# The output product of a SwiGLU as a 2 by 2 block product with seven multiplications, its partial sums kept in PSUM

## The chip, the cores and the metric

The kernel runs on one core of one Trainium2 chip. The metric is device time in microseconds (us) for one execution; the median of three executions stands for a kernel. The profile is of one more execution, so it has a time of its own.

## The reference

One decoder layer on 512 tokens of width 1024, all in float32. What matters here is the second of its two SwiGLU half steps:

```
h = h + 0.5 * swiglu(rmsnorm(h, norm_ffn2), ffn2_w1, ffn2_w3, ffn2_w2)

def swiglu(x, w1, w3, w2):
    return (silu(x @ w1) * (x @ w3)) @ w2        # w1, w3: 1024 x 2816, w2: 2816 x 1024
```

Before it come a first SwiGLU, an attention (NSA) and a state space mixer (S5); after it a gated input embedding and a last norm.

## The kernel before

**Layout.** Everything is kept transposed: `h` is 8 row tiles of 128 features by 512 tokens. The 2816 hidden features are 22 tiles (`FT_N`). A weight reaches SBUF as a *unit* of 128 by 1024 float32 (`unit`, 512 KB), which `split` (L154) divides in a high and a low part: ScalarE casts (L159), VectorE subtracts (L160). Every product is then made of three float32r matmuls, high by high, high by low, low by high (`mm3`). One matmul is a weight load of 128 by 128 and a pass of the moving operand, 256 or 512 columns (tokens). All of them are issued in one line, L134.

**Up.** Tile 0 of the second SwiGLU is computed plainly. The 21 others go through `up_fast`: seven products of half size, each 12 matmuls of 256 columns, in place of eight, with sums carried on in PSUM from a copy (L400 copies a partial sum from a bank of tag A into one of tag B, on which the next matmuls accumulate). That is 84 matmuls of 256 columns for a tile. The hidden tile (128 x 512) is written by VectorE in two halves (L423, L427), multiplied by the silu (L433) and split by `hidden` (L353 on ScalarE, L354 on VectorE) into a tile of tag `hq`, of which there are seven.

**Down.** `down` takes a group of hidden tiles (`CHUNKS`: 6, 6, 5, 5). For each of the 8 output tiles m it runs three matmuls of 512 columns for every hidden tile of the group into a bank of tag C, and L487 adds half of the bank to `h[:, m]` on VectorE. A group's `down` comes after the first `up` of the next group.

**PSUM** has eight banks of 128 x 512 float32: two each of the tags A, B, C, D, used in turn.

**Order.** Each engine executes its instructions in an order written out by hand for the whole kernel (`ENGINE_ORDER`: steps between the numbers that the instructions have in the program; `TILE_ORDER`: some reuses of tiles). `impose` turns it into dependencies. Three matmuls of one product mostly stay together, and products of neighbouring steps are mixed.

**Weights ahead.** Eight units can be in SBUF during the second SwiGLU: four of the ring and four of `fp2` (`more[:] = fp2, 4`).

Of the kernel before, what the change touches and what calls it, by code (L numbers as in the profile page):

```python
# [24 lines left out]
CHUNKS = [range(0, 6), range(6, 12), range(12, 17), range(17, 22)]  # L25
UNIT = 1024
# [10 lines left out]
def _ffn_order():  # L37

    order = []
    for c, fl in enumerate(CHUNKS):  # L40
        order.append(("up", fl[0]))
        if c:
            order.append(("down", c - 1))
        order.extend(("up", f) for f in fl[1:])
    order.append(("down", len(CHUNKS) - 1))
    return order


FFN_ORDER = _ffn_order()


def _unit_widths():

    w = []

    def ffn():
        for kind, i in FFN_ORDER:
            w.extend([UNIT, UNIT] if kind == "up" else [UNIT] * len(CHUNKS[i]))

    ffn()  # L60
    w.extend([UNIT] * 12)
    w.extend([840, 840, 560])
    w.extend([UNIT] * 8)
    w.extend([UNIT] * 2)
    w.extend([UNIT] * 8)
    w.extend([UNIT] * 2)
    ffn()
    w.extend([UNIT] * 8)
    return w
# [7 lines left out]
def block_kernel(ctx: ExitStack, tc: tile.TileContext, a: dict, out: bass.AP):  # L77
# [267 lines left out]
    def ffn(nrm, done, plain, xp, hp, fp, bg=None, first=None, restate=None):  # L345
        fast = not bg
        if True:
            hid = {}

            def hidden(f, t3):  # L350
                hq = hp.tile([128, 2, SEQ], FR, tag="hq", name="hq")
                hh, hl = hq[:, 0], hq[:, 1]
                S.copy(hh, t3)  # L353
                V.tensor_tensor(hl, t3, hh.bitcast(F32), OP.subtract)  # L354
                hid[f] = (hh, hl)
# [52 lines left out]
            def up_fast(f, after):  # L408
# [13 lines left out]
                t3 = fp.tile([128, SEQ], F32, tag="t3", name="t3")  # L422
# [13 lines left out]
            def up(f):  # L436
                if f >= plain:
                    return up_fast(f, f + 1 < FT_N and f not in [c[0] for c in CHUNKS[1:]])
# [19 lines left out]
                t3 = fp.tile([128, SEQ], F32, tag="t3", name="t3")  # L458
# [36 lines left out]

            for kind, i in FFN_ORDER:
                if kind == "up":
                    up(i)
                    aside(SMALL.get(i, int(i > 7)))
                else:  # L500
                    down(CHUNKS[i], i == len(CHUNKS) - 1)
# [847 lines left out]
    hp2 = x2.enter_context(tc.tile_pool(name="hid2", bufs=7, reuse_waits="tile"))  # L1349
# [17 lines left out]

    pled = dram.tile([D_MODEL, SEQ], F32, tag="pled", name="pled")
    norm2 = rsqrt_steps([n2.acc], 4)
    for m in range(KT):  # L1370
# [3 lines left out]
        for k in range(2):  # L1374
# [6 lines left out]
            if (m, k) == NORM_AT[1]:  # L1381
                _, pb2 = next(norm2)
                n2.spread(lambda: hp2.tile([128, 2, SEQ], F32, tag="hq", name="xn"), xpool, x2pool, pb2)
        et = fp2.tile([128, SEQ], F32, tag=("t1", "t3")[m % 2], name="et")
        S.copy(et, o)
        nc.sync.dma_start(pled[128 * m:128 * m + 128], et)
    more[:] = fp2, 4
    ffn(n2, feed_next(3), N_PLAIN, x2pool, hp2, fp2)
# [5 lines left out]
    with tc.tile_pool(name="gate", bufs=2, reuse_waits="tile") as gp:  # L1394
# [62 lines left out]
N_PLAIN = 1  # L1457
NORM_AT = (2, 0), (4, 1)
# [366 lines left out]
```

## Time and profile before

| | |
|---|---|
| median of 3 executions | 1035.49 us (1035.15 to 1035.61) |
| profiled execution | 1035.68 us |
| its span, first to last instruction | 1033.8 us |
| TensorE busy | 1017.7 us, 98% of the span |
| VectorE busy | 808.9 us, 78% |
| ScalarE busy | 522.7 us, 51% |
| mean granted TensorE clock | 0.995 of full speed |

TensorE's busy time counts overlapping matmuls once, and a matmul's duration is longer than the distance from its start to the next one's. So the distance, and not the duration, says what a matmul costs in a full stream.

### The profile page before, as it was taken

The numbers are of one execution on the slowest core, as the hardware profiler recorded it, in microseconds if no ns is written. First come the engines' busy times: TensorE is split into PE (matmuls) and PEld (weight loads), VectorE is DVE, ScalarE is ACT, GpSimd is POOL, SyncE is SP. The second block draws the span as 40 slices with busy tenths as digits, with TensorE's granted clock in tenths as the row PEclk, the third lists the DMA queues.
The fourth block names the chain that finished last, engine by engine and source line by source line (L and its number), as shares of the span: only waits on it lengthen the run. The fifth ranks groups of instructions, "written<-read, shape, count | busy, mean of one in ns | idle before, by whom it ended". The sixth has DMA issues, their size and how long they took to land.

```text
span 1033.8 us, 16693 instructions
## 1 busy us (share of the span) xinstructions
PE 1017.7 (98%) x6362; PEld 894.6 (87%) x6362; DVE 808.9 (78%) x1351; ACT 522.7 (51%) x915; POOL 82.2 (8%) x102
## 2 busy tenths in 40 slices
PE   9999999999999999999999999999999999999995
PEld 8788899889999878897687687998999899899885
DVE  7999997778897777899799979774576467476676
ACT  6364365346435521348779847552455255255452
POOL 1000111001011020000000000111011011110000
PEclk9999999999999999999999999999999999999998
DMA  8526366757755838986610174557265545544312
GB/s 312 135 73 177 78 185 164 224 125 157 212 145 123 285 101 214 279 241 143 224 41 1 25 222 120 133 149 198 62 153 155 131 116 144 149 107 119 102 62 82
DMA packets 76257, 151.66 MB, mean 147 GB/s; under 512 B 19473, under 2 KB 32913, under 8 KB 75921
## 3 DMA queue, kind: packets, MB, share of 16 engines
q1 hardware_dynamic: 63792, 130.26, 41.1%
q0 software_dynamic: 11520, 20.16, 12.1%
q8 instruction: 50, 0.82, 0.3%
q10 hardware_dynamic: 864, 0.17, 0.1%
q14 instruction: 31, 0.25, 0.1%
HBM read 123.53 MB, written 17.30 MB: 136 GB/s over the span
## 4 chain that ended last, share of the span: by engine, by line
PE 92%; DVE 4%; DMA 1%; issue 1%; ACT 0%; POOL 0%; DVEq 0%; SPq 0%; POOLq 0%
PE ps_C L134 28%; PE ps_B L134 25%; PE ps_A L134 24%; PE ps_D L134 15%; DVE lo L160 1%; DMA raw<-in_wpack 1%; DVE acc L192 1%; DVE xn L283 1%; DVE xn L298 0%; DVE xl L290 0%; DMA h<-in_xT 0%; PE ps_C L685 0%; ACT hi L159 0%; POOL ri L325 0%; PE ps_D L938 0%
## 5 line engine op out<-in xcount | busy, mean ns | idle before, releaser
L159 ACT CAST hi<-raw 128x1024 fp32r<-128x1024 f32 (+2 forms) x206 | 213.5, 1043 | 251.2 <-PE ps_C L134 95.5
L160 DVE TENSOR_TENSOR lo<-raw,hi 128x1024 fp32r<-128x1024 f32 (+2 forms) x206 | 247.2, 1211 | 57.8 <-ACT hi L159 56.1
L134 PE MATMUL ps_C<-hq,hi 128*128 128x512 f32 x704 | 218.2, 391 | 0.0
L134 PEld LDWEIGHTS ps_C<-hq,hi 128*128 128x128 f32 x704 | 127.2, 188 | 22.7 <-issue 0.2
L134 PE MATMUL ps_C<-hq,lo 128*128 128x512 f32 x352 | 137.1, 389 | 0.0
L134 PE MATMUL ps_A<-xh,lo 128*128 128x256 f32 (+1 forms) x432 | 134.1, 310 | 0.9 <-DVE lo L160 0.9
L134 PE MATMUL ps_A<-xh,hi 128*128 128x256 f32 (+1 forms) x432 | 134.6, 311 | 0.0
L134 PE MATMUL ps_A<-xl,hi 128*128 128x256 f32 (+1 forms) x432 | 134.3, 311 | 0.1
L134 PEld LDWEIGHTS ps_A<-xl,hi 128*128 128x128 f32 x432 | 81.6, 189 | 6.0 <-DVE xl L290 0.5
L134 PEld LDWEIGHTS ps_A<-xh,lo 128*128 128x128 f32 x432 | 81.7, 189 | 5.6 <-DVE lo L160 1.4
L134 PEld LDWEIGHTS ps_A<-xh,hi 128*128 128x128 f32 x432 | 81.5, 189 | 5.7 <-issue 0.5
L134 PE MATMUL ps_B<-sh,hi 128*128 128x256 f32 x304 | 85.9, 283 | 0.0
L134 PE MATMUL ps_B<-sh,lo 128*128 128x256 f32 x304 | 85.3, 281 | 0.5 <-DVE lo L160 0.5
L134 PE MATMUL ps_B<-sl,hi 128*128 128x256 f32 x304 | 85.5, 281 | 0.0
L487 DVE SCALAR_TENSOR_TENSOR h<-ps_C,h 128x512 f32<-128x512 f32 x64 | 44.1, 689 | 47.6 <-PE ps_C L134 46.9
L134 PEld LDWEIGHTS ps_C<-hq,lo 128*128 128x128 f32 x352 | 66.1, 188 | 14.2
L134 PE MATMUL ps_D<-sl,hi 128*128 128x256 f32 x236 | 66.5, 282 | 0.5 <-DVE sl L302 0.5
L134 PE MATMUL ps_D<-sh,hi 128*128 128x256 f32 x236 | 66.4, 281 | 0.0
L134 PE MATMUL ps_D<-sh,lo 128*128 128x256 f32 x236 | 66.2, 280 | 0.0
L369 POOL DMA_DIRECT2D raw<-raw x38 | 32.8, 862 | 397.0 <-DVE lo L160 364.7
L363 POOL DMA_DIRECT2D raw<-in_wpack x38 | 35.8, 942 | 300.9 <-DVE h L1122 131.1
L134 PEld LDWEIGHTS ps_B<-sh,hi 128*128 128x128 f32 x304 | 57.3, 188 | 0.9 <-ACT pu L384 0.2
(401 smaller groups left out, 2313.5 us busy)
## 6 DMA issues: line engine op xcount, KB each, us to landing
raw<-in_wpack SPq DMA_DIRECT2D x171, 512.0 KB, 4.0
raw<-in_wpack POOLq DMA_DIRECT2D x38, 256.0 KB, 5.0
raw<-raw POOLq DMA_DIRECT2D x38, 256.0 KB, 3.3
so<-s5o SPq DMA_DIRECT2D x8, 512.0 KB, 6.6
h<-in_xT SPq DMA_DIRECT2D x8, 256.0 KB, 4.9
s5f<-fs SPq DMA_DIRECT2D x4, 512.0 KB, 4.2
s5o<-gt SPq DMA_DIRECT2D x4, 512.0 KB, 3.7
s5t<-tcs SPq DMA_DIRECT2D x2, 1024.0 KB, 5.2
```

The lines of the kernel that those rows point to most:

```text
L134: return PE.matmul(o, lhsT, rhs, start=start, stop=stop, **kw)
L159: S.copy(hi[:, c], raw[:, c])
L160: V.tensor_tensor(lo[:, c], raw[:, c], hi[:, c].bitcast(F32), OP.subtract)
L192: adder.tensor_tensor(self.acc, self.acc, sq, OP.add)
L283: V.scalar_tensor_tensor(row(k), h[:, k, :], gains[:, self.gi, k:k + 1], pb, OP.mult, OP.mult)
L363: nc.gpsimd.dma_start(a0[:, 1], src[:, 0:512], accum_op=OP.add)
L369: nc.gpsimd.dma_start(a1[:, 1], a0[:, 1], accum_op=OP.add)
L487: V.scalar_tensor_tensor(h[:, m, :], o, 0.5, h[:, m, :], OP.mult, OP.add)
```

## The change

The 16 first hidden tiles of the second SwiGLU are put in four groups of four, the last six are a group as before (`CHUNKS2`).

For a group of four, `down_block` computes output tiles m and m + 4 together, as a 2 by 2 block product: rows (m, m + 4), columns of w2's input (even hidden tiles, odd ones), tokens (0 to 255, 256 to 511). It needs seven products instead of eight, each of 2 hidden tiles x 3 = 6 matmuls of 256 columns. VectorE forms three sums of weight blocks (`sw`), which are split like the weights (`v`), and one block is overwritten in place.

The hidden tiles come in pairs: `target` puts the two halves of two tiles in one tile `st`, `pair` adds four sums of them on VectorE, and the seven blocks are split together (1792 columns, one cast on ScalarE, one subtraction on VectorE) into a tile `hs` of tag `hq`. That tag has two tiles of 3584 columns in place of seven of 1024.

In PSUM a row tile uses a half bank X of tag A, a half bank W of tag D, and two banks P and Q, which are both banks of tag C and stay the same for all 16 row tiles. X is copied three times by ScalarE while it grows: into P's first half, Q's first half, P's second half, and further products are accumulated on the copies. One matmul for P and one for Q stand ahead of the first row tile. Half of W, Q, X and P is then added to `h` by four instructions of VectorE instead of two.

`begin` of the next but one hidden tile comes ahead of the group's last row tile. Weights are kept six units ahead instead of eight (`more[:] = fp2, 2`), and the temporaries of the norm before it lie in the new tiles (`spare`). `ENGINE_ORDER` and `TILE_ORDER` are new for the whole kernel.

```diff
+CHUNKS2 = [range(0, 4), range(4, 8), range(8, 12), range(12, 16), range(16, 22)]
...
+            def target(f):
+                if not nblock:
+                    return fp.tile([128, SEQ], F32, tag="t3", name="t3")
+                if f >= blocked or f % 2 == 0:
+                    keep["st"] = fp.tile([128, 7, 256], F32, tag="st", name="st", bufs=1)
+                i = 0 if f >= blocked else 2 * (f % 2)
+                return keep["st"][:, i:i + 2].rearrange("p a b -> p (a b)")
+
+            def pair(f):
+                s = keep["st"]
+                V.tensor_tensor(s[:, 4], s[:, 1], s[:, 0], OP.subtract)
+                V.tensor_tensor(s[:, 1], s[:, 3], s[:, 1], OP.subtract)
+                V.tensor_tensor(s[:, 5], s[:, 4], s[:, 3], OP.subtract)
+                V.tensor_tensor(s[:, 6], s[:, 5], s[:, 2], OP.add)
+                hs = hp.tile([128, 2, 7, 256], FR, tag="hq", name="hs")
+                S.copy(hs[:, 0], s)
+                V.tensor_tensor(hs[:, 1], s, hs[:, 0].bitcast(F32), OP.subtract)
+                hid[f - 1] = hs
...
+            def down_block(fl):
+                hs = [hid[f] for f in fl[::2]]
...
+                for m in range(mh):
+                    raw = unit(True)
+                    a_ = raw.rearrange("p (q c) -> p q c", q=4)
+                    sw = fp.tile([128, 3, 256], F32, tag=("pp", "ph")[m % 2], name="sw", bufs=1)
+                    V.tensor_tensor(sw[:, 0], a_[:, 2], a_[:, 3], OP.add)
+                    V.tensor_tensor(sw[:, 1], a_[:, 0], sw[:, 0], OP.subtract)
+                    V.tensor_tensor(a_[:, 2], a_[:, 0], a_[:, 2], OP.subtract)
+                    V.tensor_tensor(sw[:, 2], a_[:, 1], sw[:, 1], OP.add)
+                    w = split(raw)
+                    v = [fp.tile([128, 768], FR, tag=n, name=n, bufs=2) for n in ("vh", "vl")]
+                    swf = sw.rearrange("p q c -> p (q c)")
+                    S.copy(v[0], swf)
+                    V.tensor_tensor(v[1], swf, v[0].bitcast(F32), OP.subtract)
...
+                    def prod(o, u, q, slot, begin, end):
+                        for j in range(2):
+                            c = slice(256 * q + 128 * j, 256 * q + 128 * j + 128)
+                            for i, (x_, y_) in enumerate(((0, 0), (0, 1), (1, 0))):
+                                mm(o, u[x_][:, c], hs[j][:, y_, slot], begin and j + i == 0,
+                                   end and j == 1 and i == 2, skip_group_check=True)
+
+                    if m == mh - 1:
+                        for _ in begin(fl[-1] + 2):
+                            pass
+                    X, W = bank("A")[:, lo], bank("D")[:, lo]
+                    prod(X, w, 0, 0, True, True)
+                    prod(W, w, 2, 1, True, True)
+                    S.copy(P[:, lo], X)
+                    prod(X, v, 1, 5, False, True)
+                    prod(P[:, lo], w, 1, 2, False, True)
+                    S.copy(Q[:, lo], X)
+                    prod(X, v, 0, 4, False, True)
+                    prod(Q[:, lo], w, 3, 6, False, True)
+                    S.copy(P[:, hi], X)
+                    prod(P[:, hi], v, 2, 3, False, True)
+                    g = h[:, m + mh].rearrange("p (a t) -> p a t", a=2)
+                    V.scalar_tensor_tensor(g, W[:, None, :].to_broadcast([128, 2, 256]), 0.5, g, OP.mult, OP.add)
+                    for t, o in ((lo, Q[:, lo]), (hi, X)):
+                        V.scalar_tensor_tensor(h[:, m + mh, t], o, 0.5, h[:, m + mh, t], OP.mult, OP.add)
+                    V.scalar_tensor_tensor(h[:, m], P, 0.5, h[:, m], OP.mult, OP.add)
...
-    hp2 = x2.enter_context(tc.tile_pool(name="hid2", bufs=7, reuse_waits="tile"))
+    hp2 = x2.enter_context(tc.tile_pool(name="hid2", bufs=2, reuse_waits="tile"))
...
-    more[:] = fp2, 4
-    ffn(n2, feed_next(3), N_PLAIN, x2pool, hp2, fp2)
+    more[:] = fp2, 2
+    ffn(n2, feed_next(3), N_PLAIN, x2pool, hp2, fp2, None, None, None, CHUNKS2, FFN_ORDER2, NBLOCK)
```

## Rows read from the trace of the kernel before

**Rows 1.** The page's part 1: the span, and for each engine the busy time, its share of the span and its instructions.

```profile
span 1033.8 us, 16693 instructions
PE 1017.7 (98%) x6362; PEld 894.6 (87%) x6362; DVE 808.9 (78%) x1351; ACT 522.7 (51%) x915; POOL 82.2 (8%) x102
```

**Rows 2.** The waits of TensorE in the whole run, longest first: who waited for whom, us in total, times, longest.

```profile
PE ps_D L134 <- DVE dg L331: 3.3, 2, 2.6
...
PE ps_D L134 <- DVE sl L302: 0.5, 1, 0.5
PE ps_B L134 <- DVE lo L160: 0.5, 1, 0.5
...
```

**Rows 3.** Busy time of each engine in stretches of 20 us of the second SwiGLU and in the last 33.8 us: PE, PEld (weight loads), DVE, ACT, POOL, each with its instructions (x), then the granted clock, the DMA share and GB/s.

```profile
660.00:680.00 20.00, 20.00 (x169) 19.88 (x168) 15.57 (x22) 11.82 (x20) 2.62 (x3) 1.00 0.64 152
740.00:760.00 20.00, 20.00 (x171) 19.98 (x170) 17.11 (x23) 12.32 (x21) 3.52 (x4) 1.00 0.57 145
880.00:900.00 20.00, 20.00 (x98) 16.85 (x97) 9.78 (x12) 4.45 (x5) 2.60 (x3) 1.00 0.63 176
1000.00:1033.80 33.80, 22.56 (x146) 20.00 (x144) 20.84 (x45) 10.96 (x22) 1.56 (x2) 0.85 0.19 63
```

**Rows 4.** The chain that ended last, pieces of it inside the second SwiGLU: start, length in us, what. ps_C is a run of matmuls of 512 columns (`down`), ps_B and ps_D runs of 256 columns (`up_fast`).

```profile
809.41 8.18 PE ps_C L134 x36
...
857.78 2.13 PE ps_D L134 x18
859.91 2.84 PE ps_B L134 x24
...
882.14 8.87 PE ps_C L134 x39
```

**Rows 5.** VectorE's groups from 640 to 965 us by shape: line, engine, operation, out<-in, count, then busy us, mean ns of one, and the idle time before them with its releasers.

```profile
L160 DVE TENSOR_TENSOR lo<-raw,hi 128x1024 fp32r<-128x1024 f32 x85 | 102.7, 1222 | 36.8 <-ACT hi L159 36.4
L487 DVE SCALAR_TENSOR_TENSOR h<-ps_C,h 128x512 f32<-128x512 f32 x28 | 19.3, 690 | 35.2 <-PE ps_C L134 35.2
L354 DVE TENSOR_TENSOR hq<-t,hq 128x512 fp32r<-128x512 f32 x22 | 15.2, 689 | 4.8 <-ACT hq L353 4.2
L366 DVE TENSOR_TENSOR raw<-raw 128x512 f32<-128x512 f32 x21 | 14.4, 688 | 0.4
L372 DVE TENSOR_TENSOR al<-raw,ah 128x512 fp32r<-128x512 f32 x21 | 14.4, 687 | 8.6 <-ACT ah L371 8.3
L433 DVE TENSOR_TENSOR t<-t,t 128x512 f32<-128x512 f32 x21 | 14.4, 687 | 2.9 <-ACT t L432 2.8
L365 DVE TENSOR_TENSOR raw<-raw 128x512 f32<-128x512 f32 x20 | 13.8, 689 | 0.4
L423 DVE TENSOR_TENSOR t<-ps_D,pu 128x256 f32<-128x256 f32 x21 | 8.8, 421 | 10.8 <-PE ps_D L134 9.0 <-ACT pu L384 1.8
L427 DVE TENSOR_TENSOR t<-p,ps_B 128x256 f32<-128x256 f32 x21 | 8.8, 419 | 10.0 <-PE ps_B L134 9.8
```

**Rows 6.** VectorE's instructions in order of time where they follow each other without a gap (start, us, line, operation, out<-in, count of a merged run).

```profile
638.88 2.48 DVE L298 TENSOR_TENSOR xn<-xn 128x512 f32<-128x512 f32 x4
...
644.16 3.48 DVE L160 TENSOR_TENSOR lo<-raw,hi 128x1024 fp32r<-128x1024 f32 x3
...
664.59 0.42 DVE L423 TENSOR_TENSOR t<-ps_D,pu 128x256 f32<-128x256 f32 x1
664.92 2.35 DVE L160 TENSOR_TENSOR lo<-raw,hi 128x1024 fp32r<-128x1024 f32 x2
```

**Rows 7.** ScalarE's groups from 640 to 965 us, columns as in rows 5.

```profile
L159 ACT CAST hi<-raw 128x1024 fp32r<-128x1024 f32 x85 | 88.5, 1050 | 100.0 <-PE ps_C L134 56.9 <-PE ps_B L134 17.3 <-issue 16.8
L353 ACT CAST hq<-t 128x512 fp32r<-128x512 f32 x22 | 13.7, 621 | 14.0 <-DVE t L433 12.8 <-DVE t L461 1.2
...
L400 ACT COPY ps_B<-ps_A 128x256 f32<-128x256 f32 x21 | 7.6, 364 | 9.1 <-PE ps_A L134 8.9
```

**Rows 8.** Instructions in order of time around a wait of TensorE for VectorE, start and us; in brackets the idle time before and its releaser.

```profile
641.89 2.35 DVE L302 TENSOR_TENSOR sl<-xn,sh 128x1024 fp32r<-128x1024 f32 x2
...
642.38 0.28 PE L134 MATMUL ps_D<-sh,hi 128*128 128x256 f32 x1
643.16 0.19 PEld L134 LDWEIGHTS ps_D<-sl,hi 128*128 128x128 f32 x1 [0.81 <-DVE sl L302]
643.16 0.38 PE L134 MATMUL ps_D<-sl,hi 128*128 128x256 f32 x1 [0.50 <-DVE sl L302]
...
643.38 0.28 PE L134 MATMUL ps_D<-sh,lo 128*128 128x256 f32 x1
```

**Rows 9.** The last matmul of a product and the copy of its result by ScalarE, which was waiting for it.

```profile
666.76 0.28 PE L134 MATMUL ps_B<-sh,lo 128*128 128x256 f32 x1
...
667.12 0.37 ACT L384 COPY pu<-ps_B 128x256 f32<-128x256 f32 x1 [0.37 <-PE ps_B L134]
```

More of the change, by code (lines that the diff above doesn't have):

```diff
@@ L32, with _ffn_order @@
 NCH = NG // GC
-def _ffn_order():
+def _ffn_order(chunks):
     order = []
-    for c, fl in enumerate(CHUNKS):
+    for c, fl in enumerate(chunks):
         order.append(("up", fl[0]))
@@ L44, in _ffn_order, with ffn @@
         order.extend(("up", f) for f in fl[1:])
-    order.append(("down", len(CHUNKS) - 1))
+    order.append(("down", len(chunks) - 1))
     return order
-FFN_ORDER = _ffn_order()
+FFN_ORDER = _ffn_order(CHUNKS)
+FFN_ORDER2 = _ffn_order(CHUNKS2)
 def _unit_widths():
     w = []
[L56 to L60, printed above, removed]
+    def ffn(order, chunks):
+        for kind, i in order:
+            w.extend([UNIT, UNIT] if kind == "up" else [UNIT] * len(chunks[i]))
+    ffn(FFN_ORDER, CHUNKS)
     w.extend([UNIT] * 12)
@@ L66, in _unit_widths @@
     w.extend([UNIT] * 2)
-    ffn()
+    ffn(FFN_ORDER2, CHUNKS2)
     w.extend([UNIT] * 8)
@@ L342, in block_kernel, with ffn @@
     G.memset(negh, -0.5)
-    def ffn(nrm, done, plain, xp, hp, fp, bg=None, first=None, restate=None):
+    def ffn(nrm, done, plain, xp, hp, fp, bg=None, first=None, restate=None, chunks=CHUNKS, order=FFN_ORDER, nblock=0):
         fast = not bg
@@ L348, in ffn @@
             hid = {}
-            def hidden(f, t3):
-                hq = hp.tile([128, 2, SEQ], FR, tag="hq", name="hq")
+            keep = {}
+            blocked = chunks[nblock][0] if nblock else 0
+            def target(f):
[15 more added lines that the diff above has]
+                hid[f - 1] = hs
+            def hidden(f, t3):
+                if f < blocked:
+                    if f % 2:
+                        pair(f)
+                    return
+                if nblock:
+                    r = (f - blocked) % 3
+                    if r == 0:
+                        keep["hs"] = hp.tile([128, 3584], FR, tag="hq", name="hq")
+                    hq = keep["hs"][:, 1024 * r:1024 * r + 1024].rearrange("p (a t) -> p a t", a=2)
+                else:
+                    hq = hp.tile([128, 2, SEQ], FR, tag="hq", name="hq")
                 hh, hl = hq[:, 0], hq[:, 1]
@@ L421, in up_fast @@
                 t1 = fp.tile([128, SEQ], F32, tag="t1", name="t1", bufs=2 if fast else 1)
-                t3 = fp.tile([128, SEQ], F32, tag="t3", name="t3")
+                t3 = target(f)
                 V.tensor_tensor(t3[:, lo], zw, pu, OP.subtract)
@@ L437, in up @@
                 if f >= plain:
-                    return up_fast(f, f + 1 < FT_N and f not in [c[0] for c in CHUNKS[1:]])
+                    return up_fast(f, f + 1 < FT_N and f not in [c[0] for c in chunks[1:]])
                 wu = [first if f == 0 and first else unit(), unit()]
@@ L457, in up @@
                 t1 = fp.tile([128, SEQ], F32, tag="t1", name="t1", bufs=2 if fast else 1)
-                t3 = fp.tile([128, SEQ], F32, tag="t3", name="t3")
+                t3 = target(f)
                 if fast:
@@ L494, in down @@
                         aside((2 - m % 2) * (m > 4 or fl[0] > 0))
-            for kind, i in FFN_ORDER:
-                if kind == "up":
+            def down_block(fl):
+                hs = [hid[f] for f in fl[::2]]
+                if "P" not in keep:
+                    for n in "PQ":
+                        keep[n] = bank("C")
+                P, Q = keep["P"], keep["Q"]
+                mh = KT // 2
+                for m in range(mh):
[11 more added lines that the diff above has]
+                    V.tensor_tensor(v[1], swf, v[0].bitcast(F32), OP.subtract)
+                    if "C" not in keep:
+                        keep["C"] = True
+                        for o in (P, Q):
+                            mm(o, w[0][:, :128], nrm.xh[:, 0], True, True, skip_group_check=True)
+                    def prod(o, u, q, slot, begin, end):
[23 more added lines that the diff above has]
+                    V.scalar_tensor_tensor(h[:, m], P, 0.5, h[:, m], OP.mult, OP.add)
@@ L498, in ffn @@
+            for kind, i in order:
+                if kind == "down" and i < nblock:
+                    down_block(chunks[i])
+                elif kind == "up":
                     up(i)
@@ L500, in ffn @@
                 else:
-                    down(CHUNKS[i], i == len(CHUNKS) - 1)
+                    down(chunks[i], i == len(chunks) - 1)
     fd = dram.tile([128, NG, 128], F32, tag="s5f", name="s5f")
@@ L1366, in block_kernel, with spare @@
     n2 = state["n"]
+    def spare():
+        ts = [hp2.tile([128, 3584], F32, tag="hq", name="xn") for _ in range(2)]
+        ts.append(fp2.tile([128, 1792], F32, tag="st", name="xn", bufs=1))
+        views = [t[:, 1024 * r:1024 * r + 1024].rearrange("p (a t) -> p a t", a=2)
+                 for t, n in zip(ts, (3, 3, 1)) for r in range(n)]
+        views.append(views[4])
+        return lambda: views.pop(0)
     pled = dram.tile([D_MODEL, SEQ], F32, tag="pled", name="pled")
@@ L1382, in block_kernel @@
                 _, pb2 = next(norm2)
-                n2.spread(lambda: hp2.tile([128, 2, SEQ], F32, tag="hq", name="xn"), xpool, x2pool, pb2)
-        et = fp2.tile([128, SEQ], F32, tag=("t1", "t3")[m % 2], name="et")
+                n2.spread(spare(), xpool, x2pool, pb2)
+        et = fp2.tile([128, SEQ], F32, tag=("t1", "vh")[m % 2], name="et")
         S.copy(et, o)
         nc.sync.dma_start(pled[128 * m:128 * m + 128], et)
-    more[:] = fp2, 4
-    ffn(n2, feed_next(3), N_PLAIN, x2pool, hp2, fp2)
+    more[:] = fp2, 2
+    ffn(n2, feed_next(3), N_PLAIN, x2pool, hp2, fp2, None, None, None, CHUNKS2, FFN_ORDER2, NBLOCK)
     del more[:]
@@ L1457 @@
 N_PLAIN = 1
+NBLOCK = 4
 NORM_AT = (2, 0), (4, 1)
@@ L1695, in half_tiles, with quarters, ffn @@
                                 .transpose(1, 0, 2) for t, hf in zip(ws, hs)], axis=1))
-    def ffn(w1, w3, w2, plain=FT_N):
-        for kind, i in FFN_ORDER:
+    def quarters(w, fl):
+        for m in range(KT // 2):
+            add(np.concatenate([w[k * 128:(k + 1) * 128, o * 128:(o + 1) * 128]
+                                for o in (m, m + KT // 2) for ks in (fl[::2], fl[1::2]) for k in ks], axis=1))
+    def ffn(w1, w3, w2, plain, chunks, order, nblock=0):
+        for kind, i in order:
             if kind == "up" and i >= plain:
@@ L1703, in ffn @@
                 up_tile(w3, i)
-            else:
-                m_major(w2, range(KT), CHUNKS[i])
-    ffn(x["ffn1_w1"][0], x["ffn1_w3"][0], x["ffn1_w2"][0], PLAIN1)
+            elif i < nblock:
+                quarters(w2, chunks[i])
+            else:
+                m_major(w2, range(KT), chunks[i])
+    ffn(x["ffn1_w1"][0], x["ffn1_w3"][0], x["ffn1_w2"][0], PLAIN1, CHUNKS, FFN_ORDER)
     w_in = x["w_in"][0]
@@ L1735, in _pack_weights @@
     m_major(x["w_ple"][0], range(8), range(2))
-    ffn(x["ffn2_w1"][0], x["ffn2_w3"][0], x["ffn2_w2"][0], N_PLAIN)
+    ffn(x["ffn2_w1"][0], x["ffn2_w3"][0], x["ffn2_w2"][0], N_PLAIN, CHUNKS2, FFN_ORDER2, NBLOCK)
     m_major(x["w_ple_gate"][0], range(8), range(8))
```

328 rows, old and new, of tables (ENGINE_ORDER, TILE_ORDER) are left out of this document.

## The prediction

> **What bounds the kernel now.** I read the page's busy times first, then the waits of TensorE, then the second SwiGLU in slices, then the spacing of its matmuls. TensorE is busy 1017.7 of 1033.8 us [rows 1], and its longest waits are a few us outside the two SwiGLUs; in the second one only two of 0.5 us are left, both at its very start [rows 2]. From there to the end of its work TensorE fills every slice, 20.00 of 20.00 us at full clock, in the stretches of `up` and in those of `down` alike [rows 3]. So time is gained there only by a shorter stream of matmuls, and any wait that the change puts into this stream is lost one for one. The last row of [rows 3] shows the tail, where TensorE works 22.56 of 33.80 us; the change doesn't shorten it.
>
> A matmul costs its distance to the next one, not its duration. The chain gives it as a run's length by its count [rows 4]: with 512 columns 8.18 / 36 = 0.2272 us and 8.87 / 39 = 0.2274; with 256 columns 2.13 / 18 = 0.1183 and 2.84 / 24 = 0.1183. Two halves cost 0.2366, so cutting a pass in two costs 4%.
>
> **The matmuls.** Removed: for 16 hidden tiles, 8 output tiles and 3 parts, 384 matmuls of 512 columns, 384 x 0.2273 = 87.3 us. Added: 16 row tiles x 7 products x 6 matmuls = 672 of 256 columns, 672 x 0.1183 = 79.5 us, and the two that stand ahead of P and Q, of 512 columns, 0.5 us. Balance: -7.3 us. The last six hidden tiles cost 144 matmuls of 512 columns either way, and the 21 tiles of `up_fast` the same 84 each. If the distances are off by 0.0005 us in the worst direction, the balance lies between -6.8 and -7.8.
>
> **The copies of X.** This is the wait that the change adds. X can grow only when ScalarE has read it. Between the last matmul of X and the next one into X (or into the half that was copied to) stand the six of another product, in places more: counted along TensorE's new list, 30 of the 48 copies have exactly six between, the 18 others nine or more. With six, the next one is due 7 x 0.1183 = 0.83 us after X's last matmul started. The row for such a step: ScalarE's copy starts 0.36 us after the last matmul's start (666.76 to 667.12) and takes 0.37 us [rows 9]; a copy from PSUM to PSUM takes 0.364 [rows 7]. Then TensorE. Its restart after a wait is in [rows 8]: the first of VectorE's two subtractions, 1.21 us each, ends at 643.10; weight load and matmul start together at 643.16, and the next matmul comes 0.22 us later instead of 0.118. So the dependent matmul counts as started 0.06 + 0.10 = 0.16 us after its releaser. Sum: 0.36 + 0.37 + 0.16 = 0.89 us against 0.83 due: 0.06 us lost at each of the 30, 1.8 us, if ScalarE stands idle when X is complete. The bounds: 0, if the restart costs nothing because the wait is over when the weight load is due; and a cast of 1.05 us [rows 7] that has just begun on ScalarE when X is complete, for which I give a price in the rivals. In the new list most casts stand behind a copy and not between two of a row tile, so I take 1.8.
>
> P's half is another such ring: the first copy of a row tile writes where VectorE has to have read the row tile before it. P's last matmul, 0.36 us, 0.60 us on VectorE, then 0.36 for the copy and 0.16: 1.5 us, against 13 x 0.118 = 1.54 due. No loss if VectorE takes P at once.
>
> **VectorE.** Its price in a full stream is again the distance. Four of 512 columns take 2.48 us and the last of them 0.69, so (2.48 - 0.69) / 3 = 0.60; three of 1024 take 3.48, so (3.48 - 1.22) / 2 = 1.13; one of 256 is 664.59 to 664.92, 0.33 [rows 6]. About 0.07 + 0.00104 per column; by that (an estimate) 768 columns cost 0.87 and 1792 cost 1.93. An `up` tile has three of 1024, five of 512 and two of 256 [rows 5]: 3.39 + 3.00 + 0.66 = 7.05 us, in 84 x 0.1183 = 9.94 us of TensorE. After the change L354 goes (-0.60), and each pair adds four of 256 and one of 1792, 3.25 us: 8.08 us a tile on average, 9.70 on an odd one. A row tile of `down_block`: four of 256 for the sums (1.32), 1.13 and 0.87 for the splits, two of 512 and two of 256 for `h` (1.86): 5.18 us, against 42 x 0.1183 = 4.97 of TensorE. A group of four is 4 x (8.08 + 5.18) = 53.0 us of VectorE in 4 x (9.94 + 4.97) = 59.6 of TensorE: 89%. Before, the same work was 28.2 + 4.5 for the splits + 3.5 for `h` = 36.2 us in 39.8 + 21.8 = 61.6: 59%. It still fits on average, but in `down_block` and in odd tiles VectorE has no slack at all, and what it has to do there must be done early (splits go three units ahead, the tiles of `v` two). Every hold-up of VectorE by TensorE, such as the 10.8 and 10.0 us ahead of L423 and L427 [rows 5], now comes back to TensorE. The nearest row for a dense stretch is 740 to 760 us: VectorE busy 17.11 of 20 us, and TensorE without a gap [rows 3]. From it I take a small loss, 0.25 us in each of the 4 groups' joints, 1 us; bounds 0 and the rival below.
>
> **Nothing.** ScalarE: a row tile adds a cast of 768 columns and three copies to a cast that was there before; with durations that is 1.05 + 0.8 (an estimate between 0.62 for 512 and 1.05 for 1024) + 3 x 0.36 = 2.9 us of 4.97; covered, and only its order matters (above). The two tiles `hs` in place of seven `hq`: the four tiles of a group fill both, and the next pair is written only after the group's products, one `up` later; the next `up` starts with 24 matmuls (2.8 us) that need no new `st`, so TensorE has that cover. Weights: six units ahead, 512 KB each; a row tile uses one in 5 us and an `up` tile two in 10, both about 105 GB/s, where a slice of this stage carries 176 GB/s without a gap on TensorE [rows 3]. The last group has six tiles instead of five, so the norm's steps behind it (`done`) have 18 matmuls of cover instead of 15. The orders of the other stages are new too; TensorE has only 1033.8 - 1017.7 = 16.1 us idle there, most of it in the tail, so I put this at 0 with bounds of -1 and +1.
>
> **Sum.** -7.3 + 1.8 + 1.0 = -4.5 us against the profiled execution's 1035.68 us (its span of 1033.8 and 1.9 around it): 1031.2. That execution is 0.2 above the median, so 1031.0 is the forecast for the median.
>
> **The rivals.**
>
> *No new wait.* The copies hide wholly and VectorE keeps up: -7.3, so 1028.2. For it: TensorE runs without a gap in `up_fast`, which has a copy of the same kind (L400) in every tile. Against it: there twelve matmuls stand behind the copy, here six. Chance 0.24.
>
> *ScalarE's casts in the way of the copies.* If at 16 of the 48 copies (one a row tile) a cast of 1.05 us [rows 7] is half done, the copy is 0.5 us late: 8 us more than the balance, 1036.2, no change. Against it: the order of the casts in the list. Chance 0.12.
>
> *VectorE becomes the bound (the other side).* If in-order waiting keeps VectorE from being used above 84% of a group, a group lasts 53.0 / 0.84 = 63.1 us instead of 59.6, 14 us for four, and the time is 1035.5 - 7.3 + 14 = 1042. It decides from 53.0 / (59.6 + 9.4 / 4) = 86% down (the balance of 7.3 and 0.2% of the time, 2.1 us, spread over four groups). For it: the slices of `up` before had 78% and 86% [rows 3], and 89% is asked for now, in places over 100%. Against it: those slices were never short of VectorE, their idle time is mostly spare. Chance 0.14.
>
> *Half the columns, more than half the price.* If a matmul of 256 columns cost over 87.3 / 673 = 0.1297 us, or 57% of one of 512, seven products would lose to eight. [rows 4] has it at 52%, so this needs matmuls that are slower in the new place; at 0.140, say because a matmul's weights come later, it would be +7.3 us, 1043. The Trainium skill, page "TensorE: Matmul & The Clock Gate", section "Back-to-back issue gap", says that pairs of weight load and matmul settle at some 81 ns for 128 columns and 131 ns for 512; halfway by columns that makes an estimate of 98 ns for 256, 75% of one of 512, and the change would lose 15 us by it. The trace disagrees with both the level and the ratio. Chance 0.02.
>
> **The numbers.** My own case has 0.48, around 1031.0, and by its terms' bounds it runs from 1029 to 1033. Within 0.2% (2.1 us, about what a measurement of this kernel can tell from no change) ends at 1033.4 and 1037.6. Faster: 0.48 + 0.24 = 0.72. Same: 0.12 and a little of the next, 0.13. Slower: 0.15. For 8 in 10 the range goes from the case without waits and its balance of -7.8, 1027.7, to the case of the casts, 1036.5; that leaves out VectorE's and the last.
>
> **What would show it.** Right: runs of 256 columns at 0.118 us in the row tiles of P and Q; short waits of TensorE for ScalarE's copies, under 0.1 us each; VectorE busy 17 to 18.5 us in every 20 us slice of the first four groups; TensorE's instructions up by 290. Wrong: waits of TensorE for VectorE (lo, the subtraction of v, h) or for copies of several tenths each in every row tile, or slices of `up` that TensorE no longer fills.

## The result, and the profile after

The changed kernel takes 1029.87 us (median of 4, 1029.08 to 1030.10) against 1035.55 of the kernel before: 0.9943 of its time, 95% interval 0.9926 to 0.9961. The forecast was 1031.0 in a range of 1027.7 to 1036.5; the kernel is faster, by 5.7 us instead of 4.5. A second series beside the experiments gave 1029.10 (5 runs); where an experiment is compared with the changed kernel below, 1029.5 stands for it, between the two. The experiments ran on several chips, on which the kernel before took between 1035.55 and 1035.79 us.

The page's part 1 of the changed kernel, against [rows 1]:

```profile
span 1028.0 us, 17526 instructions
PE 1013.1 (99%) x6652; PEld 902.2 (88%) x6652; DVE 873.9 (85%) x1495; ACT 554.4 (54%) x971; POOL 81.9 (8%) x102
```

TensorE has 290 instructions more and 4.6 us of busy time less. VectorE has 65 us more and 144 instructions more, which come from the second SwiGLU. The span fell by 5.8 us.

Busy time in slices of the first four groups, columns as in [rows 3]:

```profile
652.00:900.00 248.00, 247.83 (x2076) 246.85 (x2075) 227.76 (x353) 147.08 (x240) 29.59 (x34) 1.00 0.54 140
660.00:680.00 20.00, 20.00 (x168) 19.84 (x168) 19.36 (x31) 13.53 (x21) 1.71 (x2) 1.00 0.56 143
680.00:700.00 20.00, 20.00 (x169) 19.96 (x169) 19.44 (x33) 10.39 (x19) 2.61 (x3) 1.00 0.73 192
700.00:720.00 20.00, 20.00 (x171) 19.98 (x170) 16.55 (x25) 10.92 (x19) 2.63 (x3) 1.00 0.38 88
720.00:740.00 20.00, 19.83 (x167) 19.51 (x165) 18.91 (x30) 14.26 (x22) 1.72 (x2) 1.00 0.57 144
```

TensorE still fills the stage: 247.83 of 248 us. VectorE is busy 227.76 of these 248 us, 92%; the same stretch of the kernel before has:

```profile
652.00:900.00 248.00, 248.00 (x1736) 232.07 (x1735) 157.21 (x201) 110.44 (x178) 28.69 (x33) 1.00 0.57 143
```

That is 63%. The row tiles of the first group run from 682 to 706 us. In that slice, and as much in the one ahead of it, where VectorE forms and splits the sums for them, it now stands at 97% (19.44 and 19.36 of 20 us), and TensorE has no gap that the slice would show. Behind the row tiles VectorE has 16.55 us. From 720 to 740 us, an `up` slice ahead of the second group's row tiles, TensorE lacks 0.17 us; the cause is shown below.

The chain of the changed kernel inside the second group, its last row tile and the start of the `up` behind it (start, length in us, what):

```profile
754.35 0.72 PE ps_A L136 x6
755.07 0.72 PE ps_D L136 x6
755.78 0.71 PE ps_A L136 x6
756.49 0.71 PE ps_C L136 x6
757.21 0.71 PE ps_A L136 x6
757.92 1.43 PE ps_C L136 x12
759.35 0.36 PE ps_A L136 x3
```

X, W, X, P, X, then Q and P: 42 matmuls from 754.35 to 759.35, 5.00 us, where 42 x 0.1183 is 4.97. To within 1% the matmuls of a row tile cost what those of `up` did.

Instructions in order of time around the first copy of the first row tile, to be held against [rows 8, 9]:

```profile
682.79 0.28 PE L136 MATMUL ps_A<-hs,lo 128*128 128x256 f32 x1
...
683.11 0.36 ACT L567 COPY ps_C<-ps_A 128x256 f32<-128x256 f32 x1 [0.61 <-PE ps_A L136]
...
683.50 0.28 PE L136 MATMUL ps_D<-sh,lo 128*128 128x256 f32 x1
683.51 0.30 PEld L136 LDWEIGHTS ps_A<-hs,vh 128*128 128x128 f32 x2
683.62 0.28 PE L136 MATMUL ps_A<-hs,vh 128*128 128x256 f32 x1
```

X's last matmul starts at 682.79; the copy starts 0.32 us later and ends at 683.47; the weight load of the next matmul into X runs at 683.51, 0.04 us after, which is when it was due anyway, ahead of its matmul at 683.62. From X's last to X's next matmul it is 0.83 us, seven distances, with nothing lost. With only six matmuls between, X's next one comes 0.83 or 0.84 us after its last throughout. It leaves nothing to spare: in two row tiles whose first copy starts 0.38 us after X's last matmul TensorE loses 0.06 us right behind, and in two more, with nine matmuls between and a later copy, as much; that is 0.25 us in all.

The other waits hang partly on VectorE, as here at the start of the third group's first row tile:

```profile
801.00 2.03 DVE L370 TENSOR_TENSOR hs<-st,hs 128x1792 fp32r<-128x1792 f32 x1 [0.29 <-ACT hs L369]
...
803.08 0.19 PEld L136 LDWEIGHTS ps_A<-hs,hi 128*128 128x128 f32 x1 [0.17 <-DVE hs L370]
```

The weight load comes 0.05 us after the subtraction that ends the pair's split. The longest wait, in which TensorE stands still for the 0.17 us that the slice above lacks, is of another kind. It lies in `up` and is for ScalarE's copy `pu`: between the last matmul into the bank that is copied and the next one the new order has only three others:

```profile
738.07 0.28 PE L136 MATMUL ps_B<-sh,lo 128*128 128x256 f32 x1
...
738.45 0.37 ACT L417 COPY pu<-ps_B 128x256 f32<-128x256 f32 x1 [0.51 <-PE ps_B L136]
...
738.87 0.19 PEld L136 LDWEIGHTS ps_B<-sh,hi 128*128 128x128 f32 x1 [0.37 <-ACT pu L417]
```

Summed over the trace from 652 us to the last `down` matmul, the distances between starts that exceed 0.1183 or 0.2273 us by more than 0.04 hold 1.9 us in excess, in 18 places; before the change it was 0.8 us in 11 places. By what released the matmul, VectorE has 0.7 of the 1.9 us, ScalarE's copies in `up` have 0.9 (0.44 at the place above), and those in the row tiles 0.25. Before the change VectorE had 0.1, the copies in `up` 0.3, and for 0.4 the trace names nobody. From the first matmul of tile 0 to the last of `down` the stage lasts 340.43 us (629.69 to 970.12) instead of 346.40 (629.43 to 975.83): 5.97 less, so the matmuls alone gave back 5.97 + 1.1, some 7.0 us.

### The profile page after: what moved, and what is told of

Same layout as the page of the kernel before. It is cut to its first block, busy times and chain, and to the rows that moved or that the text cites. A ratio compares the mean times of both kernels' runs of the same rounds, so it can differ in the third digit from the quotient of the medians.

```text
span 1028.0 us, 17526 instructions
## 1 busy us (share of the span) xinstructions
PE 1013.1 (99%) x6652; PEld 902.2 (88%) x6652; DVE 873.9 (85%) x1495; ACT 554.4 (54%) x971; POOL 81.9 (8%) x102
## 4 chain that ended last, share of the span: by engine, by line
PE 88%; issue 4%; DVE 3%; DMA 2%; ACT 2%; POOL 0%; SPq 0%; DVEq 0%; POOLq 0%; ACTq 0%
PE ps_A L136 26%; PE ps_B L136 24%; PE ps_C L136 21%; PE ps_D L136 16%; DVE lo L162 1%; DMA fi<-s5f 1%; DMA raw<-raw 1%; ACT hi L161 0%; DMA h<-in_xT 0%; DVE xl L292 0%; PE ps_C L772 0%; ACT xh L183 0%; DVE xn L300 0%; DVE xn L285 0%; DVE el L1338 0%
## 5 line engine op out<-in xcount | busy, mean ns | idle before, releaser
L136 PE MATMUL ps_C<-hq,hi 128*128 128x512 f32 x448 | 139.2, 392 | 0.0
L136 PEld LDWEIGHTS ps_C<-hq,hi 128*128 128x128 f32 x448 | 81.2, 188 | 15.4 <-DVE h L520 0.2
L136 PE MATMUL ps_C<-hq,lo 128*128 128x512 f32 x224 | 87.4, 390 | 0.0
L136 PEld LDWEIGHTS ps_B<-sl,hi 128*128 128x128 f32 x304 | 57.3, 188 | 1.1 <-DVE sl L304 0.8
L136 PEld LDWEIGHTS ps_B<-sh,lo 128*128 128x128 f32 x304 | 57.4, 189 | 0.0
```

The source lines that it names most:

```text
L136: return PE.matmul(o, lhsT, rhs, start=start, stop=stop, **kw)
```

## The experiments

**The changed kernel again**, as the measure for the next three.

> The changed kernel itself, on the same chip as the three experiments beside it, so that they have something to be compared with. All theories: 1029.5 to 1030.2 us.

Measured: 1029.10 us, 0.9935 of the kernel before (0.9922 to 0.9949), 0.4 below the range that was expected; so 0.5 us between two runs says little.

**Copies that wait for nothing.**

```diff
-                    S.copy(P[:, lo], X)
+                    S.copy(P[:, lo].rearrange("p (a t) -> p a t", a=2), ones[:, None, :].to_broadcast([128, 2, 128]))
... (Q[:, lo] and P[:, hi] likewise)
```

> The three copies of a row tile read a constant in SBUF instead of X, so nothing waits for X any more (the sums in P and Q are left out by that). Theory: the copy chain, 0.32 us from X's last matmul to the copy, 0.36 for the copy, 0.04 to the weight load of the dependent matmul, ends just where that weight load is due, so copies cost nothing: the time stays within 0.4 us of the changed kernel's, the few gaps of 0.05 to 0.25 us behind the first copies go. Rival (the prediction's term): 30 copies cost 0.06 us each, so the time falls by 1.8 us.

Measured: 1029.79 us, 0.9944 (0.9931 to 0.9956), the changed kernel's time. Without the wait for X nothing is gained, so the term of 1.8 us falls. The excess from 652 us on is again 1.9 us. Of the four small gaps behind a first copy two went (0.06 us each); at the two others TensorE now waits for VectorE's split of `v`, and for a copy that itself waits for VectorE's reading of P.

**Less work for VectorE.**

```diff
-                    V.scalar_tensor_tensor(h[:, m], P, 0.5, h[:, m], OP.mult, OP.add)
+                    V.scalar_tensor_tensor(h[:, m, 0:8], P[:, 0:8], 0.5, h[:, m, 0:8], OP.mult, OP.add)
... (the additions of W, Q and X likewise)
```

> The four additions to h of each of the 16 row tiles are made on 8 columns only (the rest of the addition is left out): 1.86 us of VectorE's work become some 0.3, 25 us less in all. Theory: VectorE is what the waits of about 2 us in the first four groups come from, since it is used nearly without a pause there; the time falls by 0.7 to 1.8 us. Rival: VectorE has slack and those gaps have other causes: within 0.3 us of the changed kernel.

Measured: 1028.98 us, 0.9938 (0.9925 to 0.9950); by the traces the stage is 0.3 us shorter. VectorE's busy time in the first four groups fell to:

```profile
652.00:900.00 248.00, 247.83 (x2078) 246.97 (x2078) 204.76 (x354) 147.00 (x241) 29.52 (x34) 1.00 0.55 141
```

23 us of VectorE's work out of the way, 83% instead of 92%, and next to nothing gained: 0.1 us by the medians of the series, 0.3 by the stage. So the rival came out, and not the theory's 0.7 to 1.8 us. The excess is still 1.5 us, and what went is the waits behind the first copies and one for the split of `v`. So at the changed kernel's load VectorE's amount of work costs little, some 0.4 us; the waits that are left hang on single chains such as that of the pair's split and of the copies in `up`.

**More work for VectorE**, behind the last split of each row tile (`extra` puts an instruction right behind the one before it and leaves the rest of the order as it is). It takes the maximum of a row tile of `h` with itself, which changes nothing.

```diff
                     V.tensor_tensor(v[1], swf, v[0].bitcast(F32), OP.subtract)
+                    for _ in range(1):      # 3 in the second run
+                        extra(lambda: V.tensor_tensor(h[:, 7], h[:, 7], h[:, 7], OP.max))
```

> One more instruction of VectorE on 512 columns (0.60 us) behind the last split of each row tile, the order otherwise kept: 9.6 us more of VectorE's work, 55.4 us in a group of 59.6 us of TensorE (93%). Theory: it fits into what VectorE has left, at the price of somewhat later splits: 0.5 to 3 us slower. Rival: VectorE is the bound of this stage already, so all of the 9.6 us shows.

> Three more instructions of VectorE on 512 columns in each row tile: 28.8 us more in all, 60.2 us in a group of 59.6 us of TensorE (101%). Theory: now VectorE is the bound: at least 2.4 us (4 groups x 0.6) slower than the changed kernel, with in-order waiting 8 to 20 us. Rival: VectorE still has slack: under 2 us.

Measured: 1034.94 us with one (0.9992, 0.9983 to 1.0001), 5.4 above the changed kernel for 9.6 us of work; 1051.54 with three (1.0149, 1.0132 to 1.0166), 22 for 28.8, somewhat over the 8 to 20 that were expected. With one instruction per row tile, 0.60 us, nearly the whole gain of the change is gone. It is more than the theory gave it and less than the rival: 56% of the added work shows at first, then 86% of what comes on top, (22.0 - 5.4) / 19.2. TensorE's waits in the run with three, from 652 us on:

```profile
PE ps_A L146 <- ACT ps_C L579: 5.0, 6, 2.0
PE ps_B L146 <- DVE st L470: 2.5, 2, 2.2
PE ps_A L146 <- DVE h L590: 2.0, 2, 1.4
PE ps_A L146 <- DVE hs L380: 1.8, 2, 1.0
PE ps_A L146 <- DVE lo L172: 1.5, 2, 1.0
```

L579 is the first copy of a row tile, whose target VectorE has read too late; the others are VectorE's directly. With one instruction the excess is 7.5 us, and some 2.5 of it stand behind first copies.

**An eighth product.**

```diff
                     prod(W, w, 2, 1, True, True)
+                    extra(lambda: prod(W, w, 2, 1, True, True))
```

> The product into W is made twice in each row tile, so there are eight products instead of seven (the result is the same): 96 matmuls of 256 columns more. Theory: TensorE's stream is the bound and each matmul costs its 0.1183 us: 11.4 us slower than the changed kernel, or 10.4 if VectorE's lateness goes with the longer stream: 1040.3 to 1041.3, slower than before the change by some 5. Rival: VectorE, not TensorE, sets the pace of the groups: under 6 us slower.

Measured: 1041.08 us (1.0050, 1.0035 to 1.0065), 11.6 above the changed kernel, and 11.2 by the traces' stage, where 11.4 was worked out. TensorE's stream sets the pace, and each matmul of 256 columns counts in full. With eight products the block scheme would lose 5 us to the kernel before.

**No cover for the first copy.** In TensorE's list, X's second product comes ahead of what is left of W's.

```diff
+        later = [i for i in w if line.index(i) > end]      # end: X's last matmul of the first product
+        at = sorted(line.index(i) for i in [*later, *x1])
+        for k, i in zip(at, [*x1, *later]):
+            line[k] = i
```

> In TensorE's order the second product into X comes right behind the first, ahead of what is left of W's product: in 12 of the 16 row tiles no other matmul stands between, in 2 three, in 2 twelve. Theory: the chain of 0.83 us (0.32 + 0.36 + 0.04 and the weight load's 0.12) then shows bare: 12 x 0.71 + 2 x 0.36 = 9.3 us slower than the changed kernel. By the prediction's chain of 0.89 us it would be 10.2. Rival: the order of the matmuls matters little, as other waits absorb it: under 3 us.

Measured: 1040.61 us (1.0046, 1.0031 to 1.0061), 11.1 above the changed kernel. The same place as above, now bare:

```profile
682.45 0.28 PE L136 MATMUL ps_A<-hs,lo 128*128 128x256 f32 x1
682.76 0.36 ACT L567 COPY ps_C<-ps_A 128x256 f32<-128x256 f32 x1 [0.61 <-PE ps_A L136]
683.17 0.30 PEld L136 LDWEIGHTS ps_A<-hs,vh 128*128 128x128 f32 x2 [0.66 <-ACT ps_C L567]
683.17 0.50 PE L136 MATMUL ps_A<-hs,vh 128*128 128x256 f32 x2 [0.45 <-ACT ps_C L567]
683.40 0.19 PEld L136 LDWEIGHTS ps_A<-hs,vl 128*128 128x128 f32 x1
683.51 0.28 PE L136 MATMUL ps_A<-hs,vl 128*128 128x256 f32 x1
```

Two matmuls start merged at 683.17 and the third at 683.51, 1.06 us after X's last instead of 3 x 0.118 = 0.35: 0.71 us for this one, as worked out. The sum is 1.8 us above the 9.3. The trace has them in other waits. In four of the bare row tiles the copy waits 0.07 us longer for VectorE's reading of P (from X's last to X's next it is then 0.79 or 0.80 us instead of 0.72). One copy in the third group, with three matmuls of cover, starts only 0.75 us after X's last and adds 0.4, and a second copy there, which waits for VectorE's reading of Q, another 0.4. A copy with twelve matmuls of cover adds 0.2, and two late splits of VectorE 0.5.

**The same extra work in other places**, to tell the place from the sum.

```diff
                 V.tensor_tensor(t3[:, lo], zw, pu, OP.subtract)
+                if f < blocked and f % 2 == 0:      # 1 in the second run
+                    for _ in range(2):
+                        extra(lambda: V.tensor_tensor(h[:, 7], h[:, 7], h[:, 7], OP.max))
```

> The extra work of VectorE stands elsewhere: two instructions on 512 columns behind the first half of each even hidden tile of the blocked groups (7 tiles, 8.4 us), where VectorE has 6.45 us of work in 9.94 us of TensorE. Theory now: what counts is the place, since VectorE has slack in the even tiles and none around the row tiles: under 2 us slower than the changed kernel. Rival: what counts is the sum over a group (93% with it, as in the run with one more in each row tile): some 5 us slower.

> The same behind the first half of each odd hidden tile (8 tiles, 9.6 us), where the pair's sums and split make 9.70 us of work in 9.94 us already. Theory (place): 4 to 9 us slower than the changed kernel. Rival (sum): some 5 us, the same as in even tiles.

Measured: 1033.88 us (0.9981, 0.9971 to 0.9990) in even tiles and 1033.89 (0.9983, 0.9973 to 0.9992) in odd ones, 4.4 above the changed kernel both times, for 8.4 and 9.6 us of work. So the sum decides far more than the place: the theory that even tiles have room falls. That VectorE's fixed order carries lateness on from tile to tile would explain it; no run separates that.

**Eight products and the extra instruction together.**

> Eight products and one more instruction of VectorE in each row tile together: VectorE 55.4 us in a group of 62.4 us of TensorE, 89% as in the changed kernel. Theory (the row tile's own balance decides: 5.78 us of VectorE against 48 x 0.1183 = 5.68 of TensorE, where the changed kernel has 5.18 against 4.97): the extra instruction is hidden now: within 1.5 us of the run with eight products alone. Rival (the extra instruction sits in the way of something, whatever the balance): 5 us or more above it, as without the eighth product.

Measured: 1041.96 us (1.0060, 1.0045 to 1.0075), 0.9 above eight products alone, or 1.6 by the traces' stage. The instruction that cost 5.4 us costs 0.9 to 1.6 once TensorE's stream is 0.71 us longer in each row tile. VectorE's share there is no higher than in the changed kernel:

```profile
652.00:900.00 248.00, 247.20 (x2064) 245.53 (x2063) 226.80 (x354) 140.10 (x230) 27.81 (x32) 1.00 0.53 135
```

226.80 us is about the 227.76 of the changed kernel. That fits the ratio of the two engines' work as what decides, but does not show it alone: the eighth product stands between X's first and second product, where it is also six more matmuls of cover for the first copy. The 2.5 us that stood behind first copies are gone altogether, while the waits for the pair's split are as long as without the eighth product (1.3 against 1.4 us). A longer stream elsewhere was not tried.

**Extra work in the kernel before.**

```diff
                 V.tensor_tensor(t3[:, lo], zw, pu, OP.subtract)
+                if nrm is not n1 and f < 16:
+                    for _ in range(2):
+                        extra(lambda: V.tensor_tensor(h[:, 7], h[:, 7], h[:, 7], OP.max))
```

> The kernel before, with two more instructions of VectorE on 512 columns behind the first half of each of the hidden tiles 1 to 15 of the second SwiGLU: 18 us more, twice what cost the changed kernel 4.4 to 5.4 us. Theory: before the change VectorE had 59% of these stretches, so it is hidden: within 0.5 us of the kernel before. Rival: an instruction put into an order written for others costs half of itself in any kernel: 9 us slower.

Measured: 1038.84 us (1.0034, 1.0020 to 1.0049), 3.3 above the kernel before for 18 us of work, neither the theory's 0 nor the rival's 9. Even at 70% (172.41 of 248 us in its trace) an instruction put into a fixed order delays something, 0.18 us for each us of work; in the changed kernel it is 0.46 to 0.56. So the prices of the runs with extra work hold such a part that is not VectorE's fullness.

## Why the prediction was right, and where it was off

**What bounds the kernel**: right. TensorE's stream does, before and after [rows 1, 3]; an added matmul shows in full (eighth product), and so does a removed one.

**The matmuls**, -7.3 us: right; 7.0 by the stage's length and its waits. The spacing of 0.118 us held in the new place, which was the condition of the rival on half the columns; that rival falls. The Trainium skill's figures, page "TensorE: Matmul & The Clock Gate", section "Back-to-back issue gap", are not what either trace shows. The traces have 227 ns for 512 columns instead of 131, and 118 for 256. (256 columns are a third of the way from 128 to 512, not half; the prediction's estimate of 98 ns is the right number for a third.)

**The copies**, +1.8 us: the term that failed. It was the small difference of two large numbers, a chain of 0.89 us against 0.83 due, and the chain measures 0.83. Some 40 of the 48 copies start 0.32 us after X's last matmul, and not the 0.36 of the one in [rows 9]; the copy takes 0.36, the weight load follows 0.04 to 0.05 later, and its matmul 0.11 after it. That is 0.72 to the weight load, which is when it is due. The lower bound of the prediction, 0 "because the wait is over when the weight load is due", was nearly the case: 0.25 us is left of the term. The run with free copies shows it in the time, the one without cover that the chain itself is real. That the chain just fits is luck: two copies that start 0.06 us later lose these 0.06 us.

**VectorE**, +1.0 us: the sum of waits came out (1.1 us more than before), but not by what was forecast. Waits for VectorE rose by 0.7 us. They stand at the joints of two of the four groups (0.22 and 0.23 us), in a row tile and in `up`, and not with 0.25 us at each joint. The other 0.4 is what waits for ScalarE's copies grew by, less the waits of before that are gone, so that the number fits is partly luck. VectorE's work was estimated at 89% of a group, and the trace has 92% busy (before, 63% against an estimate of 59%). The slices were forecast at 17 to 18.5 us of 20; they are 16.6 to 19.6, fuller where a row tile is and just ahead of it. The rival put the point from which VectorE decides at 86%: it lies higher. The changed kernel at 89% hardly pays (less work for VectorE gains 0.3 to 0.5 us), 93% costs 4.4 to 5.4 us in three different places, 101% costs 22. Of the 4.4 to 5.4 us some 1.5 to 1.8 would be the price of any instruction put into a fixed order, an estimate from the 0.18 us for each us in the kernel before. The mechanism of that rival was real, and it was a few percent of VectorE's work away.

**Nothing**: the six units ahead and the two tiles `hs` show up in no wait. ScalarE's order does: the copies in `up` cost 0.6 us more than before, 0.44 of it where the new order leaves only three matmuls between. Ahead of the stage TensorE is 0.3 us later than before, less than the profiles of the experiments differ among themselves; behind it the time is the same. TensorE's waits of the kernel before remained outside the stage, 2.8 us for the norm's `dg` among them.

So the mechanism was forecast, and the time came out 1.1 us lower mainly because the copies cost 0.25 us instead of 1.8; the matmuls gave 0.3 us less. In its copies the kernel is nearly the rival without new waits, in the sum of its other waits the case that was forecast. The upper end of the range, 1036.5, is 0.3 above the case of the casts that it names; nothing hangs on that.

## What to carry to other kernels

When an engine's stream is full, count instructions by their distance and take everything else from what the stream covers: a copy of a running sum is free where as many matmuls stand between as its chain is long, here six and with nothing to spare, and costs 0.7 us where there are none. A scheme with fewer multiplications pays in additions; work out what the adding engine has left as a share of the shorter stream, since the stream's cover shrinks while the work grows. Price a wait at the instruction that it holds up first (here the weight load), and where the price is the difference of two near numbers, give it a range and not a value. When a sum of waits comes out as forecast, ask whom each wait was for before calling the term right.

## What the runs showed of the hardware that was not expected

VectorE could be kept 97% busy over 20 us (19.36 and 19.44) while TensorE, which depends on it, lost no more than 0.2 us in either slice, and the step to visible loss is narrow: some 4% more of its work cost half a percent of the kernel's time.

A release that comes just as the next weight load is due delays its matmul by nothing (683.47 to 683.51 to the weight load, and the matmul on time at 683.62). When TensorE has stopped, the release costs 0.16 us [rows 8].
